# Start offsets of weight buffers and activation regions in SBUF, on a two-block transformer kernel

## Chip, cores, metric

The kernel runs on one core of a Trainium2 chip. The metric is the device time of one execution in microseconds, as the median over several runs. Rows of the trace come from one profiled execution.

## What is computed

Two transformer blocks follow each other on one sequence of 256 positions of width 2048, all in float32. Cut to what matters:

```python
# block 1
x = x + concat(band_attention(h), gated_linear_attention(h)) @ w_out      # h = rms_norm(x); h @ w_in first
u = causal_conv(rms_norm(x) @ w_ffn_up)                                    # 2048 -> 2 * 5632
x = x + (gelu(u_gate) * u_val) @ w_ffn_down                                # 5632 -> 2048
x = x + sigmoid(rms_norm(x) @ w_ple_gate) * (p @ w_ple_proj)
x = rms_norm(x)
# block 2: the same frame with other parts
x = x + concat(moba_attention(h), retention(h)) @ w_o_2                    # h @ w_in_2 first
x = x + (silu(h2 @ w_gate_2) * (h2 @ w_up_2)) @ w_down_2
x = x + (p_2 @ w_ple_proj_2) * sigmoid(rms_norm(x) @ w_ple_gate_2 + b)
```

Nearly all of the work is products of the activations (256 positions) with weight matrices; the core reads 464.80 MB from HBM, nearly all of it weights, each of them once.

## The kernel before

**Weight pieces.** `weight_plan` cuts all weight matrices into 881 tiles of at most 128 x 1024 float32, in the order in which they are used. Each tile passes three kinds of buffers of 4096 bytes per partition: `load` (L167) brings it by DMA into one of four `raw` buffers; `split_hi` (L175) copies it on ScalarE in the reduced format fp32r to one of five `wh` buffers; `split_lo` (L186) subtracts that on VectorE, and puts the rest into one of four `wl` buffers. `slot` does this ahead of use: when tile i is consumed, tile i+7 is loaded, i+4 split by ScalarE and i+3 by VectorE. A buffer is used again in turn, tile i taking number i modulo 4 or 5.

**Activations.** Activations of a stage stand in regions R0 to R4 (`region`), of 16384 bytes per partition each: eight k-tiles, each a high and a low part of 256 positions, so that a row of 512 numbers (2048 bytes) is one k-tile.

**Products.** Every product is taken as high by high, high by low and low by high, in fp32r matmuls (L241 records them all). In `prod_b` the weights are stationary: each 128 x 128 slice of `wh` meets the 512 columns of a k-tile, and the same slice of `wl` meets its first 256 columns. These two matmuls are called a pair below. `prod_p` works in the same direction with 256 columns. In `prod_a` the activations are stationary, and a row of the weight buffer moves: 512 columns, 256, or 272 for the tile that also holds 16 gate columns. Of 13,600 matmuls on weight buffers 11,968 have the weights stationary, and 1,632 move them.

**Addresses.** `Net.__init__` starts the weight buffers at a multiple of `ALIGN` = 2048 bytes per partition, and `t` pads so that each tile of at least 8192 bytes starts at such a multiple as well. All thirteen weight buffers and all five regions thus start at 0 within 2048. Slices of the weight buffers lie at multiples of 512 bytes, with one exception: in a 272-column tile the second row starts 1088 bytes in, which is 64 within 512.

The instruction order on each engine is written out by hand, and PSUM accumulators (`acc`) are drained a few ticks after a chunk ends.

Of the kernel before, what the change touches and what calls it, by code (L numbers as in the profile page):

```python
# [5 lines left out]
F32 = mybir.dt.float32  # L6
F32R = mybir.dt.float32r
# [5 lines left out]
P = 128  # L13
# [7 lines left out]
MIX_ORDER = (0, 1, 2, 3, 8, 9, 10, 11, 4, 5, 6, 7, 12, 13, 14, 15)  # L21
HALVES = ((0, 24), (24, 44))
ALIGN = 2048
SCRATCH = 2048


def weight_plan():

    tiles = []
    full = tuple(range(KT))

    def gemm(n, kts, chunks):
        for ch in chunks:
            for i in range(0, len(kts), n):
                tiles.append((kts[i : i + n], ch))

    def even(name, lo, hi, step):
        return [[(name, c, c + step)] for c in range(lo, hi, step)]

    def wide(name, lo, hi):
        gemm(2, full, even(name, lo, hi, 512))

    def narrow(name, lo, hi, kts=full):
        gemm(4, kts, even(name, lo, hi, 256))

    def ffn(gate, up, off, down):  # L50
        for a, b in HALVES:
            gemm(4, full, [[(gate, c * P, c * P + P), (up, off + c * P, off + c * P + P)] for c in range(a, b)])
            narrow(down, 0, D, tuple(range(a, b)))

    def ple(gate, proj):
        for c in range(0, D, 512):
            narrow(gate, c, c + 512)
            gemm(2, (0, 1), even(proj, c, c + 512, 512))

    gemm(2, full, [[("w_in", 4096, 4608)], [("w_in", 4608, 4864)], [("w_in", 4864, 5120), ("w_in", 6144, 6160)]])  # L60
    narrow("w_in", 3072, 4096)
    narrow("w_in", 0, 2048)
    wide("w_in", 2048, 3072)
    wide("w_in", 5120, 6144)
    narrow("w_out", 0, D, MIX_ORDER)
    ffn("w_ffn_up", "w_ffn_up", FF, "w_ffn_down")
    ple("w_ple_gate", "w_ple_proj")
    wide("w_in_2", 0, 3072)
    narrow("w_in_2", 3072, 5120)
    wide("w_in_2", 5120, 7168)  # L70
    narrow("w_o_2", 0, D)
    ffn("w_gate_2", "w_up_2", 0, "w_down_2")
    ple("w_ple_gate_2", "w_ple_proj_2")
    return tiles


def plan_offsets(tiles):
    out, off = [], 0
    for kts, ch in tiles:
        f = len(kts) * sum(b - a for _, a, b in ch)  # L80
        out.append((off, f))
        off += P * f
    return out, off
# [16 lines left out]
class Net:  # L100
# [4 lines left out]
    def __init__(self, nc, tc, pools, ins, out):  # L105
        self.nc, self.tc = nc, tc
        self.sp, self.wp, self.ps = pools
        self.ins, self.out = ins, out
        self.plan = weight_plan()
        self.offs, _ = plan_offsets(self.plan)  # L110
        self.i = 0
        self.raw, self.H, self.L = {}, {}, {}
        self.ev, self.side = [], []
        self.done = set()
        self.nacc = 0
        self.forced = []
        self.sizes = {}
        self.off = SCRATCH + 128
        self.pad(self.wp)
        self.off += 13 * 4096  # L120


    def t(self, tag, shape, dt=F32, bufs=1, name=None):
        size = -(-4 * int(np.prod(shape[1:])) // 32) * 32
        if tag not in self.sizes:
            if size >= 8192:
                self.pad(self.sp)
            self.sizes[tag] = size
            self.off += size * bufs
        return self.sp.tile(shape, dt, tag=tag, name=name or tag, bufs=bufs)  # L130

    def pad(self, pool):
        n = -self.off % ALIGN
        if n:
            name = f"pad{self.off}"
            pool.tile([P, n // 4], F32, tag=name, name=name, bufs=1)
            self.off += n
# [13 lines left out]
    def pv(self):  # L151
        return self.psum("pv", 1)


    def cut(self, i, part):
        f = self.offs[i][1]
        return slice(0, f) if part is None else slice(part * f // 2, (part + 1) * f // 2)

    def load(self, i, part=None):
        if i >= len(self.plan):  # L160
            return
        off, f = self.offs[i]
        if part in (None, 0):
            self.raw[i] = self.wp.tile([P, 1024], F32, tag="raw", name="raw", bufs=4)
        src = self.ins["weights"][off : off + P * f].rearrange("(p f) -> p f", p=P)
        a = self.cut(i, part)
        self.nc.sync.dma_start(self.raw[i][:, a], src[:, a])  # L167

    def split_hi(self, i, part=None):
        if i >= len(self.plan):  # L170
            return
        if part in (None, 0):
            self.H[i] = self.wp.tile([P, 1024], F32R, tag="wh", name="wh", bufs=5)
        a = self.cut(i, part)
        self.nc.scalar.activation(self.H[i][:, a], self.raw[i][:, a], AF.Copy)  # L175

    def split_lo(self, i, part=None):
        if i >= len(self.plan):
            return
        if part in (None, 0):  # L180
            self.L[i] = self.wp.tile([P, 1024], F32R, tag="wl", name="wl", bufs=4)
        a = self.cut(i, part)
        r = self.raw[i]
        if part in (None, 1):
            del self.raw[i]
        self.nc.vector.tensor_sub(self.L[i][:, a], r[:, a], self.H[i][:, a].bitcast(F32))  # L186
# [83 lines left out]
    def prod_a(self, acts, acc):  # L270
        nk = len(acts)
        for g in range(0, nk, 2):
            self.need_acts(acts[g : g + 2])
            H, L, w = self.slot(2)
            for j in range(2):
                x, _ = acts[g + j]
                for t in range(2):
                    o = acc[:, t, :w]
                    hs = slice(t * P, t * P + P)
                    ls = slice(T + t * P, T + t * P + P)  # L280
                    sl = slice(j * w, j * w + w)
                    self.mm(o, x[:, hs], H[:, sl], g + j == 0, False)
                    self.mm(o, x[:, hs], L[:, sl], False, False)
                    self.mm(o, x[:, ls], H[:, sl], False, g + j == nk - 1)
# [15 lines left out]
    def v2(self, ap):  # L300
        return ap.rearrange("p (b t) -> p b t", b=2)
# [44 lines left out]
    def acts_of(self, regions, n, key):  # L346
        return [(regions[k // 8][:, k % 8].rearrange("p a t -> p (a t)"), (key, k)) for k in range(n)]
# [1043 lines left out]
```

## Time and profile before

| | |
|---|---|
| median of 3 runs | 2562.81 us (2562.39 to 2563.21) |
| time of the profiled execution | 2564.11 us |
| span of its instructions | 2562.3 us |
| TensorE (matmul) busy | 2550.0 us, 100% of the span |
| VectorE busy | 1668.0 us, 65% |
| ScalarE busy | 1282.9 us, 50% |
| mean granted TensorE clock | 0.999 of full speed |

The span runs from the first to the last instruction. 1.8 us of the profiled execution's time lie outside it. Matmuls overlap in the trace (the next one starts before the last one's end), so the time that one costs is read from start to start, and a busy share near 100% doesn't say that the array itself is full.

### The profile page before, as it was taken

What the parts mean: (1) busy time and instruction counts of PE and PEld (TensorE: products, weight loads), DVE (VectorE), ACT (ScalarE), POOL (GpSimd) and SP (SyncE); (2) the same over time, 40 slices, a digit from 0 to 9 for tenths busy, and PEclk for the clock granted to TensorE, in tenths of its full rate; (3) what the DMA queues carried; (4) which work ended last, traced back from release to release, by engine and by line L of the source; (5) the groups of instructions that cost most, each with busy time, mean ns of one, the idle gap of its engine ahead of it and who ended that gap; (6) DMA issues with size and microseconds to landing.
All of it is one profiled execution on the core that took longest, in us unless ns stands there. A gap on an engine that the chain in (4) does not pass through costs nothing.

```text
span 2562.3 us, 36496 instructions
## 1 busy us (share of the span) xinstructions
PE 2550.0 (100%) x14162; PEld 2190.6 (85%) x14162; DVE 1668.0 (65%) x2374; ACT 1282.9 (50%) x1713; POOL 8.4 (0%) x60
## 2 busy tenths in 40 slices
PE   9999999999999999999999999999999999999999
PEld 7887788888888888888888888888888888888888
DVE  6655566777755677766786775666566555565665
ACT  6544645555543555545544644444444334444443
POOL 0000000000000000000000000000000000000000
PEclk9999999999999999999999999999999999999999
DMA  7545355555555555555555455555555555555554
GB/s 242 183 139 179 129 183 187 183 188 187 185 188 187 185 188 187 189 194 183 194 171 196 159 181 189 177 185 185 185 189 186 185 189 184 186 189 189 185 193 145
DMA packets 133550, 469.30 MB, mean 183 GB/s; under 512 B 14960, under 2 KB 17392, under 8 KB 133376
## 3 DMA queue, kind: packets, MB, share of 16 engines
q1 hardware_dynamic: 133232, 466.95, 54.6%
q8 instruction: 111, 1.82, 0.3%
q14 instruction: 63, 0.52, 0.1%
q10 hardware_dynamic: 144, 0.01, 0.0%
HBM read 464.80 MB, written 2.10 MB: 182 GB/s over the span
## 4 chain that ended last, share of the span: by engine, by line
PE 99%; DMA 0%; DVE 0%; ACT 0%; issue 0%; SPq 0%; ACTq 0%
PE acc L241 95%; PE sc L241 2%; PE pv L241 1%; PE tr L669 0%; DMA raw<-weights 0%; PE sc L1118 0%; ACT wh L175 0%; PE sc L1201 0%; PE sc L547 0%; DVE ty L967 0%; SPq L409 0%; DVE wl L186 0%; DVE X L968 0%; PE tr L756 0%; SPq L167 0%
## 5 line engine op out<-in xcount | busy, mean ns | idle before, releaser
L186 DVE TENSOR_TENSOR wl<-raw,wh 128x1024 fp32r<-128x1024 f32 (+1 forms) x881 | 1068.8, 1214 | 846.4 <-PE acc L241 547.5
L175 ACT ACTIVATE wh<-raw 128x1024 fp32r<-128x1024 f32 (+1 forms) x881 | 924.6, 1050 | 918.6 <-PE acc L241 739.8
L241 PE MATMUL acc<-f,wh 128*128 128x512 f32 x2816 | 995.7, 399 | 0.0
L241 PE MATMUL acc<-f,wl 128*128 128x256 f32 x2816 | 790.9, 281 | 0.0
L241 PEld LDWEIGHTS acc<-f,wh 128*128 128x128 f32 x2816 | 529.1, 188 | 131.9
L241 PEld LDWEIGHTS acc<-f,wl 128*128 128x128 f32 x2816 | 532.0, 189 | 0.0
L241 PE MATMUL acc<-g,wh 128*128 128x512 f32 x1408 | 497.7, 399 | 0.0
L241 PE MATMUL acc<-g,wl 128*128 128x256 f32 x1408 | 395.4, 281 | 0.0
L241 PEld LDWEIGHTS acc<-g,wh 128*128 128x128 f32 x1408 | 264.6, 188 | 66.1
L241 PEld LDWEIGHTS acc<-g,wl 128*128 128x128 f32 x1408 | 266.0, 189 | 0.0
L241 PE MATMUL acc<-hp,wh 128*128 128x512 f32 x512 | 181.3, 398 | 0.0
L241 PE MATMUL acc<-hp,wl 128*128 128x256 f32 x512 | 143.7, 281 | 0.0
L241 PEld LDWEIGHTS acc<-hp,wh 128*128 128x128 f32 x512 | 96.2, 188 | 23.2
L241 PE MATMUL acc<-wh,m2b 128*128 128x512 f32 x320 | 102.8, 393 | 0.0
L241 PE MATMUL acc<-wh,m2a 128*128 128x512 f32 x320 | 102.3, 392 | 0.0
L241 PEld LDWEIGHTS acc<-hp,wl 128*128 128x128 f32 x512 | 96.7, 189 | 0.0
L868 ACT ACTIVATE ty<-tU,vec 128x256 f32<-128x256 f32 x88 | 48.2, 595 | 75.0 <-DVE tU L864 75.0
L289 ACT ACTIVATE tq<-acc 128x512 f32<-128x512 f32 x124 | 71.8, 579 | 5.0 <-PE acc L241 5.0
L241 PE MATMUL acc<-wh,h0a 128*128 128x512 f32 (+2 forms) x224 | 68.0, 380 | 5.5 <-ACT wh L175 5.5
L241 PEld LDWEIGHTS acc<-wh,m2a 128*128 128x128 f32 x320 | 60.1, 188 | 12.3
L241 PEld LDWEIGHTS acc<-wh,m2b 128*128 128x128 f32 x320 | 60.1, 188 | 12.2
L241 PE MATMUL acc<-h0a,wh 128*128 128x512 f32 x192 | 69.2, 402 | 0.0
(272 smaller groups left out, 2784.0 us busy)
## 6 DMA issues: line engine op xcount, KB each, us to landing
raw<-weights SPq DMA_DIRECT2D x863, 512.0 KB, 3.3
raw<-weights SPq DMA_DIRECT2D x10, 256.0 KB, 2.7
raw<-weights SPq DMA_DIRECT2D x8, 272.0 KB, 2.8
aB<-bias SPq DMA_DIRECT2D x8, 256.0 KB, 3.9
X<-xT SPq DMA_DIRECT2D x7, 256.0 KB, 6.8
dk<-decay SPq DMA_DIRECT2D x8, 192.0 KB, 3.6
out<-X SPq DMA_DIRECT2D x6, 256.0 KB, 2.8
pr<-pT SPq DMA_DIRECT2D x2, 256.0 KB, 4.6
```

What stands on the lines that cost most here:

```text
L175: self.nc.scalar.activation(self.H[i][:, a], self.raw[i][:, a], AF.Copy)
L186: self.nc.vector.tensor_sub(self.L[i][:, a], r[:, a], self.H[i][:, a].bitcast(F32))
L241: self.nc.tensor.matmul(out, lhsT, rhs, start=start, stop=stop, skip_group_check=True, **kw)
L289: self.nc.scalar.activation(m, acc[:, :, T:], AF.Copy)
L868: nc.scalar.activation(y[:, b, :], u[:, b, 0:T], AF.Identity, scale=self.col("cw0", j), bias=self.col("b_ffn_conv", j))
```

## The change

Each of the thirteen weight buffers becomes a tile of its own name (`rawA` to `rawD`, `whA` to `whE`, `wlA` to `wlD`) and is placed, with padding, at a chosen offset within 2048 bytes: 0 for all four `raw`; 0, 32, 64, 128 and 1024 for `wh`; 0, 32, 64 and 96 for `wl`. The regions are placed at 0 (R0), 32 (R1), 64 (R3), 128 (R4) and 1024 (R2). Tile i still takes buffer i modulo 4 or 5. Small tiles behind these move by the padding; the last one ends at 225,696 bytes per partition. No instruction is added, removed or moved: on every engine the same instructions stand in the same order with the same semaphores waited for, and only names and addresses differ.

```diff
--- before.py
+++ after.py
@@ -21,6 +21,7 @@
 MIX_ORDER = (0, 1, 2, 3, 8, 9, 10, 11, 4, 5, 6, 7, 12, 13, 14, 15)
 HALVES = ((0, 24), (24, 44))
 ALIGN = 2048
+RESIDUE = {"R0": 0, "R1": 32, "R3": 64, "R4": 128, "R2": 1024}
 SCRATCH = 2048
 
 
@@ -116,21 +117,25 @@
         self.forced = []
         self.sizes = {}
         self.off = SCRATCH + 128
-        self.pad(self.wp)
-        self.off += 13 * 4096
+        self.offsets = {}
+        for tag, n, res in (("raw", 4, (0,) * 4), ("wh", 5, (0, 32, 64, 128, 1024)), ("wl", 4, (0, 32, 64, 96))):
+            for j in range(n):
+                self.pad(self.wp, res[j])
+                self.wtile(tag, j, F32)
+                self.off += 4096
 
 
     def t(self, tag, shape, dt=F32, bufs=1, name=None):
         size = -(-4 * int(np.prod(shape[1:])) // 32) * 32
         if tag not in self.sizes:
             if size >= 8192:
-                self.pad(self.sp)
+                self.pad(self.sp, RESIDUE.get(tag, 0))
             self.sizes[tag] = size
             self.off += size * bufs
         return self.sp.tile(shape, dt, tag=tag, name=name or tag, bufs=bufs)
 
-    def pad(self, pool):
-        n = -self.off % ALIGN
+    def pad(self, pool, residue=0):
+        n = (residue - self.off) % ALIGN
         if n:
             name = f"pad{self.off}"
             pool.tile([P, n // 4], F32, tag=name, name=name, bufs=1)
@@ -150,6 +155,11 @@
 
     def pv(self):
         return self.psum("pv", 1)
+
+    def wtile(self, tag, j, dt):
+        n = {"raw": 4, "wh": 5, "wl": 4}[tag]
+        name = tag + "ABCDE"[j % n]
+        return self.wp.tile([P, 1024], dt, tag=name, name=name, bufs=1)
 
 
     def cut(self, i, part):
@@ -161,7 +171,7 @@
             return
         off, f = self.offs[i]
         if part in (None, 0):
-            self.raw[i] = self.wp.tile([P, 1024], F32, tag="raw", name="raw", bufs=4)
+            self.raw[i] = self.wtile("raw", i, F32)
         src = self.ins["weights"][off : off + P * f].rearrange("(p f) -> p f", p=P)
         a = self.cut(i, part)
         self.nc.sync.dma_start(self.raw[i][:, a], src[:, a])
@@ -170,7 +180,7 @@
         if i >= len(self.plan):
             return
         if part in (None, 0):
-            self.H[i] = self.wp.tile([P, 1024], F32R, tag="wh", name="wh", bufs=5)
+            self.H[i] = self.wtile("wh", i, F32R)
         a = self.cut(i, part)
         self.nc.scalar.activation(self.H[i][:, a], self.raw[i][:, a], AF.Copy)
 
@@ -178,7 +188,7 @@
         if i >= len(self.plan):
             return
         if part in (None, 0):
-            self.L[i] = self.wp.tile([P, 1024], F32R, tag="wl", name="wl", bufs=4)
+            self.L[i] = self.wtile("wl", i, F32R)
         a = self.cut(i, part)
         r = self.raw[i]
         if part in (None, 1):
```

## Rows read from the trace of the kernel before

**Rows 1.** The page: span, then busy time, share and instructions of each engine.

```profile
span 2562.3 us, 36496 instructions
PE 2550.0 (100%) x14162; PEld 2190.6 (85%) x14162; DVE 1668.0 (65%) x2374; ACT 1282.9 (50%) x1713; POOL 8.4 (0%) x60
```

**Rows 2.** The page: the chain that ended last, share of the span by engine.

```profile
PE 99%; DMA 0%; DVE 0%; ACT 0%; issue 0%; SPq 0%; ACTq 0%
```

**Rows 3.** All waits of TensorE: waiter, releaser, total us, times, longest us.

```profile
PE acc L241 <- ACT wh L175: 5.5, 2, 4.7
PE pv L241 <- ACT rfb L362: 1.0, 1, 1.0
PE acc L241 <- DVE wl L186: 0.8, 1, 0.8
```

**Rows 4.** Pieces of that chain in time: start us, us, what, instructions.

```profile
...
3.06 6.67 DMA raw<-weights
9.76 1.07 ACT wh L175
10.85 1.24 DVE wl L186
...
39.02 2.88 PE acc L241 x24
...
444.67 740.59 PE acc L241 x4192
...
1344.20 19.06 PE acc L241 x84
...
1725.32 740.59 PE acc L241 x4192
```

**Rows 5.** Busy time by engine in two feed-forward stretches (first line names the columns).

```profile
core 0: us, PE busy (x) PEld busy (x) DVE busy (x) ACT busy (x) POOL busy (x), PEclk, DMA share, GB/s
444.67:1185.26 740.59, 740.59 (x4194) 642.16 (x4194) 513.18 (x676) 391.38 (x509) 4.33 (x42) 1.00 0.56 187
1725.32:2465.91 740.59, 740.59 (x4194) 642.26 (x4194) 438.35 (x494) 341.88 (x420) 0.00 (x0) 1.00 0.56 187
```

**Rows 6.** Timeline, TensorE and its weight loads: start us, us, engine, operation, operands.

```profile
1199.96 0.40 PE L241 MATMUL acc<-hp,wh 128*128 128x512 f32 x1
1200.20 0.28 PE L241 MATMUL acc<-hp,wl 128*128 128x256 f32 x1
1200.31 0.40 PE L241 MATMUL acc<-hp,wh 128*128 128x512 f32 x1
...
1199.96 0.19 PEld L241 LDWEIGHTS acc<-hp,wl 128*128 128x128 f32 x1
1200.20 0.19 PEld L241 LDWEIGHTS acc<-hp,wh 128*128 128x128 f32 x1
1200.32 0.19 PEld L241 LDWEIGHTS acc<-hp,wl 128*128 128x128 f32 x1
```

**Rows 7.** Timeline, TensorE: matmuls on the 272-column tiles (columns as before).

```profile
46.52 0.29 PE L241 MATMUL acc<-wl,h0a 128*128 128x272 f32 x1
...
51.04 0.29 PE L241 MATMUL acc<-wl,h0a 128*128 128x272 f32 x1
```

**Rows 8.** Groups by line and shape, ScalarE and VectorE: count, busy us, mean ns, idle before.

```profile
L175 ACT ACTIVATE wh<-raw 128x1024 fp32r<-128x1024 f32 x863 | 913.0, 1059 | 909.3 <-PE acc L241 733.8 <-issue 135.5 <-ACT wh L175 18.3
L333 ACT ACTIVATE tq<-X 128x512 f32<-128x512 f32 x49 | 30.4, 621 | 11.8 <-DVE X L974 10.2 <-DVE sq L338 1.6
L330 ACT ACTIVATE sq<-X 128x512 f32<-128x512 f32 x6 | 3.7, 620 | 0.8 <-DVE X L974 0.8
L186 DVE TENSOR_TENSOR wl<-raw,wh 128x1024 fp32r<-128x1024 f32 x863 | 1056.4, 1224 | 836.8 <-PE acc L241 541.1 <-issue 158.0 <-ACT g L848 102.9
L864 DVE TENSOR_TENSOR tU<-tU,rb 128x512 f32<-128x512 f32 x44 | 30.5, 692 | 1.5
L338 DVE TENSOR_TENSOR sq<-sq,tq 128x512 f32<-128x512 f32 x42 | 28.8, 685 | 0.3
```

**Rows 9.** DMA issues: tile, queue, count, KB each, median us from issue to landing.

```profile
raw<-weights SPq DMA_DIRECT2D x863, 512.0 KB, 3.3
```

## The prediction

> **What bounds the kernel now.** I read the page first, then the chain that ended last, the waits of TensorE, the long pieces of that chain, and last the timeline of single matmuls. On the page TensorE is busy for 2550.0 of 2562.3 us [rows 1], and the chain is TensorE for 99% [rows 2]. All its waits for another engine come to 5.5 + 1.0 + 0.8 = 7.3 us, nearly all before the first matmuls [rows 3]. So the end is set by how fast matmul follows matmul, and the question is whether an address can change that.
>
> The rate is read from long pieces of the chain, in which nothing else stands. 4192 matmuls of the first feed-forward take 740.59 us [rows 4], 176.67 ns each, or 353.3 ns for a pair of 512 and 256 columns. In the direction in which the weights move, 24 matmuls of 256 columns take 2.88 us, 120.0 ns each, and 84 of 512 take 19.06 us, 226.9 ns each [rows 4]. The difference, 106.9 ns for 256 columns, is 0.418 ns per column: one column per cycle at 2.4 GHz, the upper level of the clock, and the granted clock is 1.00 in these stretches [rows 5]. What is left is a fixed part per matmul: 120.0 - 256 x 0.417 = 13.3 ns there, and (353.3 - 768 x 0.417) / 2 = 16.7 ns in the pairs. Weighted by 11,968 matmuls of the one direction and 1,632 of the other, it is 16.3 ns over 13,600 matmuls, or 221 us of the span. That fixed part is the only pool from which an address could draw much.
>
> How fine this is to judge: one nanosecond on each weight matmul is 13.6 us, 0.53%. Times within 0.2%, which is 5.1 us or 0.38 ns per matmul, are what a measurement of this kernel can't tell from no change. One array cycle (0.417 ns) on all of them would already be 5.7 us.
>
> **The change part by part.**
>
> *Names instead of one tag with several buffers.* The turn of the buffers stays as it was, and so do order and waits on each engine. Nothing is added; cost 0.
>
> *DMA.* The four `raw` buffers keep offset 0, so the 863 large transfers of 512 KB and 3.3 us [rows 9] write to rows that begin as before. The few small constants that now begin elsewhere are loaded once, while TensorE has work. Cost 0; the first transfer, on the path until 9.7 us [rows 4], goes to an unmoved offset.
>
> *ScalarE and VectorE.* A split takes 1059 ns on ScalarE and 1224 ns on VectorE [rows 8]. Eight pairs, one full tile, take TensorE 8 x 353.3 = 2827 ns, and the splits run four and three tiles ahead. A split could double and TensorE would not wait. Only the first tile's two splits lie bare on the path, 1.07 and 1.24 us [rows 4]; a few per cent of them would be under 0.1 us. That offsets matter little to these engines has rows of its own: squares written to a buffer at 128 within 2048 (`tq`) take 621 ns, to one at 0 (`sq`) 620; a VectorE addition over offsets 0 and 128 takes 685 ns, a multiplication over buffers at 512, 544, 576 and 1600 takes 692 [rows 8]. Cost 0, bounds ±0.1 us.
>
> *TensorE against the other engines.* If their accesses hindered TensorE, it would be slower where they do more. In the two feed-forward stretches VectorE is busy for 513.18 and 438.35 us and ScalarE for 391.38 and 341.88 us, and the 4192 matmuls take 740.59 us in both [rows 4, 5]. The response to 124 us of extra work is below 0.01 us. Nor could start offsets keep two engines apart: TensorE passes 512 numbers in about 240 ns [rows 6], VectorE 1024 in 1224 [rows 8], so they slide along each other from any start. Gain 0, loss 0.
>
> *TensorE against itself.* Here alone two streams keep a fixed relation: the weight load for the next matmul starts together with the present one (1200.20 and 1200.20 us, 1199.96 and 1199.96 us) and lasts 0.19 us [rows 6]. Before, both addresses are 0 within 512 in all but 48 of the 13,600 matmuls. After, counted over the program, moving and stationary operand differ within 512 in 9,364; the moving one is off a multiple of 128 in 6,120 and the stationary one in 7,672. So if equal low addresses cost something now, most matmuls are freed; if uneven starts cost something, about half of them pay.
>
> The 48 exceptions are the nearest row. In the 272-column tiles six of twelve matmuls move a row that starts 64 past a multiple of 512, and the other six one that starts at 0. From 46.52 to 51.04 us lie three whole tiles, 36 matmuls [rows 7]: 125.6 ns each. The rule from the even starts gives 272 x 0.417 + 13.3 = 126.7. So an uneven start (one off a multiple of 128) neither removes the fixed part nor adds to it visibly. If the whole difference of 1.1 ns belongs to the six uneven ones, they gain 2.2 ns each; if the even six hide as much, the uneven ones lose up to that (an estimate, since their split isn't visible at the timeline's 10 ns). Carried over to the 9,364 matmuls, the bounds are -20.6 and +20.6 us. I take 0, since the average lies on the rule within one per cent, and it is the same rule for 256 and 512 columns.
>
> The Trainium skill, "TensorE: Matmul & The Clock Gate", section "Back-to-back issue gap", gives N / 2.4 + 2.5 ns for a gap, 325 ns for a pair here; no row reaches that, and by it there would be 28 ns per pair that something takes. The same page, section "Step-by-step: what each phase is for", says that TensorE reads moving operand and weights through two independent SBUF ports, so that a load takes nothing from the running matmul. By the first, freeing 9,364 matmuls would save an estimated 131 us (2432); by the second, 0.
>
> **Sum.** Removed 0, added 0, moved 0. The profiled execution stays at its 2564.11 us (span 2562.3 and 1.8 around it [rows 1]), which stands 1.3 us above the median of the runs. For the median I say 2562.8 us.
>
> **The rivals.**
>
> *Faster: collisions of TensorE's two reads go away.* For it: the fixed part is large, and before nearly every load and stream agree in the low nine bits. Against it: the uneven half of the 272-column tiles shows 125.6 ns on average and not some 120. Price: from 20.6 us by that bound (2542) to the entire fixed part of the 9,364, 9,364 x 16.3 = 153 us (2410), should offset 32 do what 64 doesn't.
>
> *Slower: an uneven start costs TensorE cycles.* A moving operand that begins at 32 or 64 would take one more fetch at its start or its end. For it: before, practically all fp32r operands are even, so the trace hardly shows the other case. Against it: the same 272-column rows. It decides from 5.1 us / 6,120 = 0.84 ns, two array cycles per uneven moving operand, on. At the bound of 2.2 ns it costs 6,120 x 2.2 = 13.5 us (2576), and with the uneven weight loads, for 9,364, 20.6 us (2583).
>
> *The change doesn't do what it says.* The allocator might have placed the buffers otherwise; the built program has them at the stated offsets, so this holds no chance of its own.
>
> **How the numbers follow.** No change: 0.80, as two independent rows (equal stretches under unequal side work, and the uneven tiles) speak for it. Slower 0.12, somewhat above the faster rival's 0.08, since only offset 64 has a row, and 32 or 96 could be less even to TensorE. The likeliest case gives 2562.8 within 0.2%, 2557.7 to 2567.9. From the rivals I take in their near ends, one cycle or two in the mean, and a little more upward: 2556 to 2571. The far ends (2410 to 2542, 2576 to 2583) are left out, and hold less than 2 in 10.
>
> **What would show it.** In the profile after, the two long pieces of 4192 matmuls should again take 740.59 us to within a few tenths, both of them, though the first reads regions at 0 and 32 on its way up and the second at 1024 and 64. Splits should stay at 1059 and 1224 ns, and waits of TensorE at about 7 us. Wrong would be: pairs other than 353.3 ns, and above all a difference between pieces that read R0 or R2 and those that read R1, R3 or R4; that would be the uneven start. A change that shows alike in all regions would point at the weight loads. Longer splits with a TensorE that waits would show that the cover was thinner than the eight pairs per tile say.

## The result, and the profile after

The changed kernel takes 2545.86 us (median of 3 runs, 2545.57 to 2545.93) against 2562.81 us: 16.95 us less, a ratio of 0.9934 with a 95% interval of 0.9911 to 0.9956. The profiled execution took 2545.93 us. The forecast was 2562.8 us and no change; the measured time lies below its range of 2556 to 2571, on the side of the first rival, and near that rival's lesser price of 2542 us.

The page of the changed kernel, its span and busy times, answers to [rows 1]:

```profile
span 2544.1 us, 36496 instructions
...
PE 2531.9 (100%) x14162; PEld 2185.4 (86%) x14162; DVE 1667.9 (66%) x2374; ACT 1283.5 (50%) x1713; POOL 8.4 (0%) x60
```

VectorE and ScalarE are as busy as before to 0.6 us. TensorE is busy for 18.1 us less, and that is the difference of the spans, 2562.3 - 2544.1 = 18.2 us. So nothing was hidden or uncovered; the matmuls themselves follow each other faster. TensorE's waits for other engines, the list of all its waits, are what they were [rows 3]:

```profile
PE acc L251 <- ACT whA L185: 5.2, 1, 5.2
PE pv L251 <- ACT rfb L372: 1.0, 1, 1.0
PE acc L251 <- DVE wlB L196: 0.8, 1, 0.8
PE acc L251 <- ACT whB L185: 0.2, 1, 0.2
```

Where the time came from is seen in the same pieces of the chain as in [rows 4], first start, then duration in us, engine and line (L251 is the L241 of before), number of instructions:

```profile
37.63 2.84 PE acc L251 x24
...
442.05 732.80 PE acc L251 x4192
...
1334.19 19.46 PE acc L251 x84
...
1716.57 731.82 PE acc L251 x4192
```

The two stretches of 4192 matmuls lost 7.79 and 8.77 us, 349.6 and 349.1 ns per pair in place of 353.3. The 84 matmuls that move 512 columns of weights went the other way, from 19.06 to 19.46 us. Busy times within the two stretches (columns as in [rows 5]) show that side work has no part in it: VectorE still differs by 75 us between them, with the two only 1 us apart.

```profile
442.05:1174.85 732.80, 732.80 (x4195) 641.12 (x4194) 513.18 (x676) 391.59 (x509) 4.33 (x42) 1.00 0.56 189
1716.57:2448.39 731.82, 731.82 (x4194) 640.62 (x4194) 438.41 (x494) 342.35 (x420) 0.00 (x0) 1.00 0.55 189
```

In the long stretches the pair time is no longer one number. The timeline of the changed kernel in the second stretch shows it, starts of the 512-column matmuls alone:

```profile
1727.54 0.39 PE L251 MATMUL acc<-f,whA 128*128 128x512 f32 x1
...
1730.27 0.39 PE L251 MATMUL acc<-f,whB 128*128 128x512 f32 x1
...
1733.06 0.39 PE L251 MATMUL acc<-f,whC 128*128 128x512 f32 x1
...
1735.89 0.39 PE L251 MATMUL acc<-f,whD 128*128 128x512 f32 x1
```

The tile in `whA` with `wlC` and region R3 (`wh` at 0, `wl` at 64, region at 64) starts at 1727.54 and is done at 1730.27 us: eight pairs in 2.73 us, 341 ns each. The tile in `whC` with `wlA` and region R2 (`wh` at 64, `wl` at 0, region at 1024) runs from 1733.06 to 1735.89, eight pairs in 2.83 us, 354 ns each. Same instructions, same shapes, five microseconds apart. The trace keeps starts to the nanosecond. Worked out from those of the 699 tiles of eight pairs that nothing interrupts, and leaving out the first two pairs of a tile, the average over pairs is 349.4 ns (353.3 in the kernel before), with averages of single tiles from 340.0 to 355.0. Tiles with the same three offsets mostly have the same rhythm (a repeating series of pair times): eleven tiles with (region 64, wh 0, wl 64) all settle at 340.0; all fifteen with (0, 0, 0) at the old one, with pairs of 350, 361 and 349 ns in turn. But 52 of the 699 lie more than 1 ns off the middle of their combination: of twelve tiles with (1024, 0, 0), eight run at 347.0 and four at 353.3.

In sum: some 3.8 ns on 5,900 pairs is about 22 us won, and 4.1 ns on some 1,380 matmuls that move 512 columns of weights (227.7 to 231.8 ns on average) 5.6 us lost. That makes about 16 of the 17.0 us.

### The profile page after: what moved, and what is told of

It reads as the page before. It is cut to its first block, busy times and chain, and to the rows that moved or that the text cites. A ratio compares the mean times of both kernels' runs of the same rounds, so it can differ in the third digit from the quotient of the medians.

```text
span 2544.1 us, 36496 instructions
## 1 busy us (share of the span) xinstructions
PE 2531.9 (100%) x14162; PEld 2185.4 (86%) x14162; DVE 1667.9 (66%) x2374; ACT 1283.5 (50%) x1713; POOL 8.4 (0%) x60
## 4 chain that ended last, share of the span: by engine, by line
PE 99%; DMA 0%; DVE 0%; ACT 0%; issue 0%; SPq 0%; ACTq 0%
PE acc L251 95%; PE sc L251 2%; PE pv L251 1%; PE tr L679 0%; DMA rawB<-weights 0%; PE sc L1128 0%; PE sc L1211 0%; PE sc L557 0%; DVE ty L977 0%; SPq L419 0%; DVE wlB L196 0%; ACT whB L185 0%; ACT whC L185 0%; DVE X L978 0%; PE tr L766 0%
## 5 line engine op out<-in xcount | busy, mean ns | idle before, releaser
L251 PE MATMUL acc<-f,whB 128*128 128x512 f32 x568 | 201.8, 394 | 0.0
L251 PE MATMUL acc<-f,whA 128*128 128x512 f32 x568 | 200.6, 393 | 0.0
L251 PE MATMUL acc<-f,whD 128*128 128x512 f32 x560 | 199.6, 395 | 0.0
L251 PE MATMUL acc<-f,whC 128*128 128x512 f32 x560 | 199.4, 395 | 0.0
L251 PE MATMUL acc<-f,whE 128*128 128x512 f32 x560 | 198.5, 394 | 0.0
L251 PE MATMUL acc<-f,wlA 128*128 128x256 f32 x704 | 197.5, 281 | 0.0
L251 PE MATMUL acc<-f,wlC 128*128 128x256 f32 x704 | 197.0, 280 | 0.0
L251 PE MATMUL acc<-f,wlB 128*128 128x256 f32 x704 | 197.0, 280 | 0.0
L251 PE MATMUL acc<-f,wlD 128*128 128x256 f32 x704 | 196.8, 280 | 0.0
L251 PEld LDWEIGHTS acc<-f,wlB 128*128 128x128 f32 x704 | 132.6, 188 | 0.0
L251 PEld LDWEIGHTS acc<-f,wlA 128*128 128x128 f32 x704 | 132.6, 188 | 0.0
L251 PEld LDWEIGHTS acc<-f,wlC 128*128 128x128 f32 x704 | 132.6, 188 | 0.0
L251 PEld LDWEIGHTS acc<-f,wlD 128*128 128x128 f32 x704 | 132.4, 188 | 0.0
L251 PEld LDWEIGHTS acc<-f,whB 128*128 128x128 f32 x568 | 106.6, 188 | 24.6
L251 PEld LDWEIGHTS acc<-f,whA 128*128 128x128 f32 x568 | 106.6, 188 | 24.4
L251 PEld LDWEIGHTS acc<-f,whC 128*128 128x128 f32 x560 | 105.1, 188 | 24.9
L251 PEld LDWEIGHTS acc<-f,whD 128*128 128x128 f32 x560 | 105.2, 188 | 24.6
L251 PEld LDWEIGHTS acc<-f,whE 128*128 128x128 f32 x560 | 105.2, 188 | 24.4
L251 PE MATMUL acc<-g,whC 128*128 128x512 f32 x288 | 102.5, 395 | 0.0
L251 PE MATMUL acc<-g,whD 128*128 128x512 f32 x288 | 102.2, 394 | 0.0
L251 PE MATMUL acc<-g,whB 128*128 128x512 f32 x280 | 99.5, 394 | 0.0
L251 PE MATMUL acc<-g,whE 128*128 128x512 f32 x280 | 99.2, 393 | 0.0
```

The lines of the kernel that those rows point to most:

```text
L251: self.nc.tensor.matmul(out, lhsT, rhs, start=start, stop=stop, skip_group_check=True, **kw)
```

## Experiments

Four theories stood against each other at first. A: TensorE's reads of moving operand and weights hinder each other depending on the difference of their addresses. B: the start address of an operand in itself is cheap or dear. C: TensorE is freed from accesses of other engines to the buffers. N: the single names did it. A fifth, D, is A as it was widened after the run with all at 32, described under "Difference or start": the differences set which steady rhythms there are, and the way into a stretch picks one. Some expectations below name it before its run is told. All diffs are against the changed kernel, and no kernel leaves out any work. Each ratio is to the kernel before, run beside it on the same chip.

### Which of the buffers

Weight buffers alone, and regions alone:

```diff
-RESIDUE = {"R0": 0, "R1": 32, "R3": 64, "R4": 128, "R2": 1024}
+RESIDUE = {}
```

> Weight buffers at the offsets of the change, all regions at 0. Theory A: the tiles whose region stood at 0 in the changed kernel show what this gives, on average 350.1 ns per pair where all-zero gives 353.3; 3.15 ns over some 5,900 pairs is 18.6 us, less some 2 to 5 us that the weights-moving direction loses: 2544 to 2549. Theory B with the moving operand as the cause: only the 1,632 matmuls that move weights change, 2560 to 2566. Theory C: near the change, 2546.

```diff
-        for tag, n, res in (("raw", 4, (0,) * 4), ("wh", 5, (0, 32, 64, 128, 1024)), ("wl", 4, (0, 32, 64, 96))):
+        for tag, n, res in (("raw", 4, (0,) * 4), ("wh", 5, (0,) * 5), ("wl", 4, (0,) * 4)):
```

> Regions at the offsets of the change, all weight buffers at 0 under single names. Theory A: by the tiles of the changed kernel that had wh and wl at 0, weighted by region, 350.2 ns per pair, 18 us gained, less what the weights-moving direction loses: 2544 to 2550. Theory B with the moving start as cause: R1, R3 and R4 gain alike, R0 and R2 nothing. Theory C: the writes of the splits are back at 0, so the gain is gone, 2561 to 2564.

Weights alone took 2543.30 us, 0.9923 of before (0.9907 to 0.9940); regions alone 2548.05 us, 0.9942 (0.9928 to 0.9957). Either half brings about what both bring together, so the halves don't add up. Theory A had worked that out from single tiles; for the weights its range, 2544 to 2549 us, was just missed. The chain of the kernel with weights moved:

```profile
441.63 731.38 PE acc L251 x4192
...
1332.26 19.43 PE acc L251 x84
...
1714.28 731.36 PE acc L251 x4192
```

Both stretches fall, 349 ns per pair, though all regions are at 0 again. That is against B with moving operands as the cause. It is against C too in the case of the regions, where the split buffers are back at 0 and the gain is still there. The chain with the regions moved:

```profile
441.73 731.07 PE acc L251 x4192
...
1713.56 735.80 PE acc L251 x4192
```

By region, B's form for this run fails as well, as R1, R3 and R4 don't gain alike: in the starts, tiles with R1 (32) run at 346.7 ns per pair, with R4 (128) at 351, and with R3 (64) at 353.3 as before. And tiles with R0, whose three offsets are 0 as before, run at 346.7 ns in 118 of 166 cases and at 353.3 in the rest. So some 6 us of this kernel's gain come from tiles whose own offsets didn't change; such a second rhythm is the subject of "Difference or start".

Names alone, with both edits above together, and the `raw` buffers alone, which ScalarE and VectorE read but TensorE never does:

> Single names and the new layout, but every weight buffer and region at 0 within 2048. The run with all at 32 showed that equal offsets have two steady rhythms, 353.3 ns per pair (before) and 346.7 ns, and that a whole feed-forward stretch of some 295 tiles falls into one of them, worth 15.6 us a stretch. Theory D (the offsets set which rhythms there are, and the entry into a stretch picks one): 2562.8, 2547 or 2532 us, nothing between. Theory N (the names, through waits or the order of buffers, bring the gain): near 2546 with pair times spread as in the changed kernel. If the rhythm of before belongs to the offset 0 itself: 2562.8 in every run.

```diff
-RESIDUE = {"R0": 0, "R1": 32, "R3": 64, "R4": 128, "R2": 1024}
+RESIDUE = {}
...
-        for tag, n, res in (("raw", 4, (0,) * 4), ("wh", 5, (0, 32, 64, 128, 1024)), ("wl", 4, (0, 32, 64, 96))):
+        for tag, n, res in (("raw", 4, (0, 32, 64, 128)), ("wh", 5, (0,) * 5), ("wl", 4, (0,) * 4)):
```

> Only the raw buffers are moved, to 0, 32, 64 and 128; wh, wl and regions stay at 0. TensorE never reads raw; the DMA writes it, ScalarE and VectorE read it. Theory D (difference of TensorE's own two addresses): the slow rhythm of 353.3 ns as before, 2562.8 us, or by another entry 2547 or 2532. Theory C (TensorE against the other engines): some of the gain appears with pair times that differ from tile to tile, 2550 to 2560.

Names alone: 2562.47 us, 0.9998 (0.9989 to 1.0007). `raw` alone: 2563.15 us, 1.0003 (0.9994 to 1.0013). Both have the old stretches to the hundredth, 740.59 us each time; the chain with names alone:

```profile
443.88 740.59 PE acc L251 x4192
...
1724.52 740.59 PE acc L251 x4192
```

So N falls, and so does C for the input side of the splits. What counts is among the buffers that TensorE reads itself.

### Difference or start

All that TensorE reads at one offset, so that every difference is 0 as before; first 32, then 64 (`S8b` holds, among other things, the embedding that `prod_p` multiplies with the weights):

```diff
-RESIDUE = {"R0": 0, "R1": 32, "R3": 64, "R4": 128, "R2": 1024}
+RESIDUE = {"R0": 32, "R1": 32, "R2": 32, "R3": 32, "R4": 32, "S8b": 32}
...
-        for tag, n, res in (("raw", 4, (0,) * 4), ("wh", 5, (0, 32, 64, 128, 1024)), ("wl", 4, (0, 32, 64, 96))):
+        for tag, n, res in (("raw", 4, (0,) * 4), ("wh", 5, (32,) * 5), ("wl", 4, (32,) * 4)):
```

> Every weight buffer that TensorE reads and every region starts at 32 within 2048; the raw buffers and X stay at 0. Theory A (TensorE's two reads, the moving operand and the next weight load, collide depending on the difference of their addresses): all differences are 0 as before, so 2562.8 us within 1 us, pairs of 353.3 ns. Theory B (an uneven start is in itself cheaper, or a start at 0 within 2048 in itself dearer): pairs leave 353.3 ns in all tiles, total near or below the 2545.9 of the change. Theory C (TensorE is freed from collisions with what ScalarE and VectorE write and read): their streams now start at 32 and 0 where all were at 0, so some of the 17 us appears, 2550 to 2560.

```diff
-RESIDUE = {"R0": 0, "R1": 32, "R3": 64, "R4": 128, "R2": 1024}
+RESIDUE = {"R0": 64, "R1": 64, "R2": 64, "R3": 64, "R4": 64, "S8b": 64}
...
-        for tag, n, res in (("raw", 4, (0,) * 4), ("wh", 5, (0, 32, 64, 128, 1024)), ("wl", 4, (0, 32, 64, 96))):
+        for tag, n, res in (("raw", 4, (0,) * 4), ("wh", 5, (64,) * 5), ("wl", 4, (64,) * 4)):
```

> All regions and all wh and wl at 64: differences 0 once more. Theory D with an entry that picks the rhythm: pairs of 353.3 or 346.7 ns alone, whole feed-forward stretches in one of them, 2562.8, 2547 or 2532 us. If starts off 0 as such bring the fast rhythm (32 did in at least one stretch): 2532 in all runs.

The first was a miss of theory A as it stood. All at 32 took 2532.03, 2544.66, 2546.55 and 2546.55 us in its four executions, 0.9920 of before by their median (0.9895 to 0.9945). The chain of the profiled one, that of 2532.03 us:

```profile
341.55 94.30 PE acc L251 x544
...
442.29 726.62 PE acc L251 x4192
...
1707.11 726.62 PE acc L251 x4192
```

Both long stretches run at 726.62 us, 346.7 ns per pair, a second rhythm (pairs of 347, 347 and 346 ns) that no tile average in the long stretches of before shows. After its first microseconds the kernel repeats the start-to-start times of the old one within a few nanoseconds, up to eight transposes (L557) that end at 318.66 us. Behind them the two go different ways, and from 341.55 us on this one runs in the fast rhythm until other work comes between. Two stretches at 346.7 ns and not at 353.3 are worth 28 us, the two of 544 before them another 3.6 us; 2562.8 less 31.6 is 2531.2, close to the 2532.03 measured. With one of the two long ones alone it is 2545 with the shorter stretches and 2549 without, and near these its other three executions lie; no trace of them was kept.

All at 64 shows that a start off 0 doesn't bring the fast rhythm by itself. Ten executions have a median of 2560.61 us, 0.9988 (0.9975 to 1.0001); nine lie from 2559.09 to 2562.47, and one at 2545.73, about where one long stretch in the fast rhythm would put it. The profiled one, 2559.09 us, which is none of the three totals expected, has the fast rhythm in the stretches of 544 (94.30 in place of 96.10 us, 3.6 us in all) and the slow one in the long stretches:

```profile
340.72 94.30 PE acc L251 x544
...
441.56 740.58 PE acc L251 x4192
...
1720.32 740.58 PE acc L251 x4192
```

So equal offsets allow two steady rhythms, and how a stretch is entered picks one of them. Theory A had to be widened to that (theory D in the expectations): the differences set which rhythms there are, the entry picks. What in the entry picks is open; before, and in the two kernels above with all at 0, the long stretches have the slow one in the traces and, by their times, in all other executions.

Now the relation that had run at 340 ns in single tiles, everywhere, and then moved as a whole by 64:

```diff
-RESIDUE = {"R0": 0, "R1": 32, "R3": 64, "R4": 128, "R2": 1024}
+RESIDUE = {"R0": 64, "R1": 64, "R2": 64, "R3": 64, "R4": 64, "S8b": 64}
...
-        for tag, n, res in (("raw", 4, (0,) * 4), ("wh", 5, (0, 32, 64, 128, 1024)), ("wl", 4, (0, 32, 64, 96))):
+        for tag, n, res in (("raw", 4, (0,) * 4), ("wh", 5, (0,) * 5), ("wl", 4, (64,) * 4)):
```

> All regions at 64, all wh at 0, all wl at 64. In the changed kernel the tiles with just these three offsets ran at 340.0 ns per pair, the shortest of its hundred combinations and without spread. Theory A: every pair with stationary weights comes to 340 ns, 13.3 ns less over some 5,900 pairs, 78 us gained, and the weights-moving direction changes by up to plus 10 us: 2480 to 2500. Theory B: uneven regions are one class, so no better than the changed kernel's average over regions at 64, 347.8 ns per pair, 2530. Theory C: the split buffers stand at two offsets only, so not better than the change, 2546 or above.

```diff
-RESIDUE = {"R0": 0, "R1": 32, "R3": 64, "R4": 128, "R2": 1024}
+RESIDUE = {"R0": 128, "R1": 128, "R2": 128, "R3": 128, "R4": 128, "S8b": 128}
...
-        for tag, n, res in (("raw", 4, (0,) * 4), ("wh", 5, (0, 32, 64, 128, 1024)), ("wl", 4, (0, 32, 64, 96))):
+        for tag, n, res in (("raw", 4, (0,) * 4), ("wh", 5, (64,) * 5), ("wl", 4, (128,) * 4)):
```

> The one relation that ran at 340 ns, shifted as a whole by 64: regions at 128, wh at 64, wl at 128. Theory D, that the difference of addresses decides: 340 ns per pair again, 2495 us within 3. Theory B, that the start itself decides (64 for regions, 0 for wh): another rhythm, 347 to 353 ns, 2525 to 2565 us.

One relation: 2495.22 us, 0.9736 (0.9721 to 0.9750). Shifted (regions 128, wh 64, wl 128): 2496.32 us, 0.9738 (0.9722 to 0.9755). The two long stretches of the first, columns as in [rows 5]:

```profile
436.95:1149.62 712.67, 712.67 (x4194) 630.88 (x4194) 513.21 (x676) 391.13 (x509) 4.33 (x42) 1.00 0.60 195
1687.26:2399.93 712.67, 712.67 (x4194) 630.90 (x4194) 438.50 (x494) 342.24 (x420) 0.00 (x0) 1.00 0.60 194
```

Each lost 27.92 us; 712.67 us are 340.0 ns per pair, again with 75 us more of VectorE's work beside the first, which speaks against C. The chain of the shifted one has the same numbers:

```profile
437.44 712.67 PE acc L251 x4192
...
1688.48 712.67 PE acc L251 x4192
```

That is against B: for this relation a start at 0 or 64, 64 or 128 makes no difference as long as the differences stay. Weights that move are dearer in both, 234.1 ns per matmul of 512 columns on average against 227.7 before.

### The two halves of that relation

Only `wl` at 64, then only the regions at 64, with everything else at 0:

```diff
-RESIDUE = {"R0": 0, "R1": 32, "R3": 64, "R4": 128, "R2": 1024}
+RESIDUE = {}
...
-        for tag, n, res in (("raw", 4, (0,) * 4), ("wh", 5, (0, 32, 64, 128, 1024)), ("wl", 4, (0, 32, 64, 96))):
+        for tag, n, res in (("raw", 4, (0,) * 4), ("wh", 5, (0,) * 5), ("wl", 4, (64,) * 4)):
```

> Only the wl buffers at 64, everything else at 0. The tiles with just this relation (0, 0, 64) ran at 346.5 ns in the changed kernel and with the weights moved alone, in every tile and with hardly a spread. Theory D: 6.7 ns less on some 5,900 pairs, 39 us, less up to 6 us in the weights-moving direction: 2520 to 2532 us. Theory B, with regions as the cause: 2562.8.

```diff
-RESIDUE = {"R0": 0, "R1": 32, "R3": 64, "R4": 128, "R2": 1024}
+RESIDUE = {"R0": 64, "R1": 64, "R2": 64, "R3": 64, "R4": 64, "S8b": 64}
...
-        for tag, n, res in (("raw", 4, (0,) * 4), ("wh", 5, (0, 32, 64, 128, 1024)), ("wl", 4, (0, 32, 64, 96))):
+        for tag, n, res in (("raw", 4, (0,) * 4), ("wh", 5, (0,) * 5), ("wl", 4, (0,) * 4)):
```

> All regions at 64, all weight buffers at 0: the other half of the 340 ns relation alone. Theory D: the tiles with (64, 0, 0) ran at 353.3 ns when regions were moved alone, so nothing is gained there, and the weights-moving direction can lose up to 8 us: 2560 to 2572 us. Theory B, with uneven regions as the cause of the gain: 347 ns, 2525 us.

`wl` alone: 2530.56 us, 0.9872 (0.9857 to 0.9887). Regions alone: 2570.35 us, 1.0030 (1.0019 to 1.0040), slower than before. Their chains, `wl` alone first:

```profile
440.99 726.62 PE acc L251 x4192
...
1707.53 726.62 PE acc L251 x4192
```

```profile
444.85 740.59 PE acc L251 x4192
...
1369.28 19.60 PE acc L251 x84
...
1731.31 740.59 PE acc L251 x4192
```

726.62 us are 346.7 ns per pair; with the regions alone it is the 353.3 of before, though in another rhythm (349, 356 and 355 ns), and the matmuls that move weights pay. Yet with `wl` moved, moving the regions as well takes it on to 340 ns. Neither operand has a good offset of its own here. An offset can also cost: the same 64 that helps in one place makes the kernel slower in another.

### Other differences, and the best kernel

Other offsets, in steps of 32 within 512, a hundred combinations in one run:

```diff
-ALIGN = 2048
-RESIDUE = {"R0": 0, "R1": 32, "R3": 64, "R4": 128, "R2": 1024}
+ALIGN = 512
+RESIDUE = {"R0": 0, "R1": 64, "R2": 192, "R3": 288, "R4": 384}
...
-        for tag, n, res in (("raw", 4, (0,) * 4), ("wh", 5, (0, 32, 64, 128, 1024)), ("wl", 4, (0, 32, 64, 96))):
+        for tag, n, res in (("raw", 4, (0,) * 4), ("wh", 5, (0, 160, 256, 320, 448)), ("wl", 4, (0, 160, 256, 352))):
```

> Regions at 0, 64, 192, 288 and 384, wh at 0, 160, 256, 320 and 448, wl at 0, 160, 256 and 352, all within 512: a hundred pairs of differences, most of them not seen yet, in one run. Theory D: steady rhythms between 340 and 354 ns, tiles of equal differences alike; a rhythm under 340 would show that the 340 of regions 64, wh 0, wl 64 is not the floor. Sum some 2535 to 2555 us.

One run of 2543.61 us. Averages of its tiles, worked out from starts, lie from 340.0 to 354.6 ns, so 340 is the floor of what was seen. Tiles with the region at 0, wh at 448 and wl at 0 (the same differences as 64, 0 and 64, modulo 512) settle at 340 ns in fourteen of fifteen cases; the last stays at 350, a second rhythm here as well. Four with wl at 256 in place of 0 settle at 340 too.

Last, both directions at their best: the differences of 340 ns for stationary weights, and for tiles whose weights move a further 64 bytes inside the `wh` buffer, which brings the difference there back to 0.

```diff
-ALIGN = 2048
+ALIGN = 512
...
-                self.off += 4096
+                self.off += 4160 if tag == "wh" else 4096
...
-        return self.wp.tile([P, 1024], dt, tag=name, name=name, bufs=1)
+        return self.wp.tile([P, 1040 if tag == "wh" else 1024], dt, tag=name, name=name, bufs=1)
...
-            self.H[i] = self.wtile("wh", i, F32R)
+            kts, ch = self.plan[i]
+            o = 16 if len(kts) == 2 and "ple_proj" not in ch[0][0] else 0
+            self.H[i] = self.wtile("wh", i, F32R)[:, o : o + 1024]
```

Offsets are those of the one relation.

> Regions at 64, wh at 0, wl at 64 within 512, and tiles whose weights move lie 64 bytes further inside the wh buffer, so that there moving weights and loaded activations differ by 0 as before the change. Theory D: pairs with stationary weights stay at 340 ns, and matmuls of 512 columns that move weights go back from 234.1 to 227.7 ns; 6.4 ns on some 1,350 of them is 8.7 us below the 2495.2 us of the run with one relation: 2486 us within 2. If only the stationary direction obeys differences: 2495.

2486.92 us, 0.9706 (0.9691 to 0.9721): 75.9 us below the kernel before and 58.9 below the changed one, the fastest of all. Its chain:

```profile
434.42 712.67 PE acc L253 x4192
...
1325.80 19.09 PE acc L253 x84
...
1678.36 712.67 PE acc L253 x4192
```

Weights that move are back at 19.09 us for 84, and the long stretches stay at 712.67.

## Why the prediction was wrong

**What held.** TensorE sets the end, and only its matmul rate could move the time. Names, DMA, ScalarE and VectorE cost nothing: names alone and `raw` alone gave 0.9998 and 1.0003. TensorE against the other engines is nothing as well, and the argument from two equal stretches under unequal side work was right; it holds again at 712.67 us. The place that the prediction named as the only one with a fixed relation, TensorE against itself, is the place.

**The step that failed** is the one behind it, "the 48 exceptions are the nearest row". The 272-column tiles belong to the direction in which weights move, and their 125.6 ns were carried over to pairs with stationary weights. In the weights-moving direction equal offsets already were the best case of those run, for 512 columns: 227.7 ns there rose to 231.8 with the change and to 234.1 with the one relation, and came back to 227.7 with the difference at 0. Against the first rival the row is quoted wrongly as well: the 125.6 ns are the average of both halves of these tiles, not of the uneven one. The trace splits them: to the nanosecond, over all eight tiles of before, the matmuls at 0 take 124.8 ns and those at 64 take 126.5. So the row showed a loss of 1.7 ns, and it could show no gain, whatever was to be had elsewhere. The term taken as 0 measured about -22 us for the pairs and +5.6 us for the moved weights. The bounds of 20.6 us to both sides were about right in size, but by luck; one relation for all pairs went to -68 us.

**A row that spoke for the rival was read and passed over.** The prediction worked out a fixed part of 13.3 ns per matmul in one direction and 16.7 ns in the other, and took both as given. Two matmuls at 13.3 would make the pair 346.7 ns, which is also the average of the second rhythm of equal offsets; the best relation even takes 6.7 ns more off. Whether that is more than a coincidence no run shows. The excess of the pairs was in the rows of before, and so was the second rhythm itself, in its short stretches. Three of them in the chain of the kernel before:

```profile
438.57 5.65 PE acc L241 x32
...
1185.70 5.56 PE acc L241 x32
1191.70 5.56 PE acc L241 x32
```

These are 16 pairs each of the same form with all offsets at 0, one at 353 ns per pair and two at 348; in the starts, the tiles of the last two settle at 347, 347 and 346 ns. So the same form already ran at two rates before any offset was moved. The chance of 0.80 rested on two rows that don't vary the thing in question for the pairs: equal stretches answer only for the other engines, and the uneven tiles belong to the other direction. For the rest all differences are multiples of 512, one case seen 13,552 times.

**The rivals.** The first came true in kind. In the changed kernel its price, 17 us, fell short of the least it was given, 20.6 us, because 5.6 us went back on moved weights; the best kernel, 2486.92 us, lies inside the span of 2542 to 2410. The second, that an uneven start costs cycles, is false as worded: shifted by 64 as a whole, nothing changes. But a slower kernel through offsets exists, 1.0030 with the regions alone. The sign named for it, pieces with R0 or R2 unlike the others, can't tell start from difference, since moving a region changes both.

The Trainium skill, "TensorE: Matmul & The Clock Gate", section "Step-by-step: what each phase is for", says that loading the next weights takes no SBUF read bandwidth from the running matmul. Here the same loads and matmuls took 340.0 or 353.3 ns per pair depending on the two streams' addresses, so in these runs the two are not independent, and the measurement decides. That page's section "Back-to-back issue gap" gives N / 2.4 + 2.5 ns as the gap of an isolated matmul; the 325 ns for a pair, an estimate from it, were reached by no run.

**What stays open.** That the differences of the addresses decide which rates there are is shown, by shifting all of them together and by moving each part. Which of the three differences (`wh`, `wl` and region against each other) does what isn't separated, as either half of the best relation alone gives another rate than both. Which part of the memory or of TensorE holds the two reads up, why the best differences seen are 0 (or 256) for `wl` and -64 for `wh` against the region, and what picks the rhythm on entering a stretch, was not settled.

## What to carry to other kernels

Where TensorE is busy throughout, compare its start-to-start times between directions and shapes before calling the remainder fixed: an excess of a few nanoseconds per matmul that only one form shows is a lead, and so are two rates of one form. Bound an unknown cost from a row of the same form, and ask whether the rows of before vary the thing in question at all. Then place operands on purpose: one kernel with many offsets shows in its timeline which combination is best, and that combination used everywhere brought four times what the mixture brought.

## What the hardware showed that was not expected

In this kernel the matmul rate depends on the differences between the start addresses of moving and stationary operands: 340.0, 346.7 or about 353 ns for a pair of 512 and 256 columns, and the best relation, shifted as a whole by 64 bytes, stays at 340.0. Equal addresses have two self-sustaining rhythms, 353.3 and 346.7 ns, that last for stretches of hundreds of tiles. Which one is entered can differ between executions of one kernel, which then scatter by 14 us (2532.03 against 2546.55) or 17 (all at 64), where those of the other kernels agree within 0.4 to 4.1 us.
